# First block's attention: the two score halves of a unit in turn, transposes a unit ahead of values, decay rates held back

## The chip, the core and the metric

The kernel runs on one core of one Trainium2 chip. TensorE multiplies (PE in the profile; PEld is its weight load), VectorE (DVE), ScalarE (ACT) and GpSimd (POOL) work on tiles, SyncE (SP) issues most DMAs. The metric is the device time of one execution in microseconds, as a median of runs.

## What is computed

Two transformer-like blocks over 256 tokens (plus 256 context tokens), in float32. The change touches the first block's attention, which is differential attention with four heads of two 64-wide halves each:

```python
def one_block(q_blk):
    s = jnp.einsum('bhcqd,bhckd->bhcqk', q_blk, k_all).astype(jnp.float32) * scale
    p = jax.nn.softmax(s, axis=-1)
    a = p[:, :, 0] - lam * p[:, :, 1]
    return jnp.einsum('bhqk,bhkd->bhqd', a.astype(v_all.dtype), v_all)
```

The index c is the half (0 or 1). The first block has two layers; layer 0 runs queries of context (256 keys) and of tokens (512 keys), layer 1 those of tokens alone. The change also touches `log_a = -LRU_C * r * jax.nn.softplus(-lam)` of the second block, of which the kernel makes a small constant, the decay rates, ahead of time.

## The kernel before

Every float32 operand of a large product is split into a high and a low part, and `mm3` (L359 to L361) adds three products: high by high, high by low, low by high. Weights come by DMA into `wraw` (four buffers), and `weights` splits them: the high part on ScalarE (L349), the low part on VectorE (L350). The modulation vectors of layer 0 are made from `wmod` weights (two buffers, L337) in steps of products on TensorE (L513); `fill` puts two steps behind each of the first twelve attention units.

A unit of attention is one head and one tile of 128 queries. `scores` takes each half c in turn: its 64 rows of qT and kT are the contraction, so half 0 lies on partitions 0 to 63 and half 1 on 64 to 127. For a half, `mm3` writes one of the two score banks ("sc"), VectorE takes the row maximum (L702), ScalarE the exponential and its sum (L704) into a tile `e` (four buffers). `values` then combines the halves on VectorE (L711 to L713), transposes the result on TensorE (L716), copies it on ScalarE to `aT` (L718), multiplies it by v (L721; each of its float32 products is two instructions), and scales the output (L725, L726). `finish` normalises a head (L732 to L738). The loop calls `scores` of the next unit before `values` of this one. `each` follows every unit: eight taps of the convolution on VectorE (L820), a fill, and now and then a pooling job.

Layer 0 calls `attention` once a head (four units), layer 1 once for two heads (two tiles each, four units); while layer 0's first units run, projections of later heads run too. The order of instructions on each engine isn't the order of the program: a scheduler goes by readiness and priority, and `tc.issue_after(x)` holds instructions behind x in it. `decay` (L920 to L924, with `log_sigmoid` L904 to L915) is called in the hidden stage of layer 1, after tile 10 of 22.

Of the kernel before, what the change touches and what calls it, by code (L numbers as in the profile page):

```python
# [14 lines left out]
AF = mybir.ActivationFunctionType  # L15
ALU = mybir.AluOpType
AX = mybir.AxisListType
# [260 lines left out]
def tile_two_blocks(ctx: ExitStack, tc: tile.TileContext, w: bass.AP, blk: bass.AP, cols: bass.AP,  # L278
# [61 lines left out]
    def weights(key):  # L340
        t, kt, n = raw_chunk(key)
        hi = whi.tile([128, CHUNK], F32R, name="whi")
        lo = wlo.tile([128, CHUNK], F32R, name="wlo")
        m = kt * n
        P["count"] += 1
        if P["both"] and P["count"] % 2:
            dve.tensor_copy(hi[:, :m], t[:, :m])
        else:
            act.copy(out=hi[:, :m], in_=t[:, :m])  # L349
        P["split"] = dve.tensor_tensor(lo[:, :m], t[:, :m], hi[:, :m].bitcast(F32), op=ALU.subtract)  # L350
        v = lambda a: a[:, :m].rearrange("p (k c) -> p k c", k=kt)
        return v(hi), v(lo)
# [5 lines left out]
    def mm3(ps, a, b, start, stop):  # L358
        pe.matmul(ps, a[0], b[0], start=start, stop=False)  # L359
        pe.matmul(ps, a[0], b[1], start=False, stop=False)  # L360
        P["product"] = pe.matmul(ps, a[1], b[0], start=False, stop=stop)  # L361
# [4 lines left out]
    def bank(p):  # L366
        return P[p].tile([128, 512], F32, name="ps_" + p)
# [4 lines left out]
    def st(n=8):  # L372
        return P["wk"].tile([128, n], F32, name=f"st{n}", bufs=8 if n < 64 else 3)
# [313 lines left out]
    def attention(l, h0, qT, kT, v, o, qts, mix, each):  # L687

        lam, sub = coef[l][:2]
        q0 = qts[0]  # L690

        def scores(j, tt):
            nk = 256 if tt < 2 else 512
            mx, s = st(2), st(2)
            e = []
            for c in range(2):
                r = slice(c * 64, c * 64 + 64)
                ps = bank("sc")
                qs = slice((tt - q0) * 128, (tt - q0) * 128 + 128)
                mm3(ps[:, :nk], (qT[j][0][r, qs], qT[j][1][r, qs]), (kT[j][0][r, :nk], kT[j][1][r, :nk]),  # L700
                    True, True)
                dve.tensor_reduce(mx[:, c:c + 1], ps[:, :nk], axis=AX.X, op=ALU.max, negate=True)  # L702
                x = P["wk"].tile([128, 512], F32, name="e", bufs=4)
                act.activation(x[:, :nk], ps[:, :nk], AF.Exp, bias=mx[:, c:c + 1], accum_out=s[:, c:c + 1])  # L704
                e.append(x)
            return nk, s, e

        def values(j, tt, ss, nk, s, e):
            h = h0 + j
            r, cc = st(2), st(1)  # L710
            dve.reciprocal(r, s)  # L711
            dve.scalar_tensor_tensor(cc, s[:, 0:1], r[:, 1:2], lam, op0=ALU.mult, op1=ALU.mult)
            dve.scalar_tensor_tensor(e[0][:, :nk], e[1][:, :nk], cc, e[0][:, :nk], op0=ALU.mult, op1=ALU.add)  # L713
            pt = bank("aux")
            for i in range(nk // 128):
                pe.transpose(pt[:, i * 128:i * 128 + 128], e[0][:, i * 128:i * 128 + 128], ident)  # L716
            aT = P["wk"].tile([128, 512], F32, name="aT", bufs=2)
            act.copy(out=aT[:, :nk], in_=pt[:, :nk])  # L718
            po = bank("aux")
            for i in range(nk // 128):  # L720
                pe.matmul(po[:, :128], aT[:, i * 128:i * 128 + 128], v[i][:, h * 128:h * 128 + 128],  # L721
                          start=(i == 0), stop=(i == nk // 128 - 1))
            q = P["wk"].tile([128, 128], F32, name="sq128")
            i = tt - q0
            act.activation(q, po[:, :128], AF.Square, scale=r[:, 0:1], accum_out=ss[:, i:i + 1])  # L725
            dve.tensor_scalar(o[tt][:, h * 128:h * 128 + 128], po[:, :128], r[:, 0:1], None, op0=ALU.mult)  # L726

        def finish(j, ss):
            h = h0 + j
            n = len(qts)  # L730
            c = slice(h * 128, h * 128 + 128)
            dve.tensor_scalar(ss[:, :n], ss[:, :n], 1.0 / 128, EPS, op0=ALU.mult, op1=ALU.add)  # L732
            rsqrt(ss[:, :n], n)
            for i, tt in enumerate(qts):
                dve.scalar_tensor_tensor(o[tt][:, c], o[tt][:, c], ss[:, i:i + 1], sub, op0=ALU.mult, op1=ALU.mult)
            pt = bank("aux")
            for i, tt in enumerate(qts):
                pe.transpose(pt[:, i * 128:i * 128 + 128], o[tt][:, c], ident)  # L738
            m = slot()
            split(pt[:, :n * 128], m[0][:, :n * 128], m[1][:, :n * 128])  # L740
            mix[h] = m

        units = [(j, tt) for j in range(len(qT)) for tt in qts]
        sums = {j: st(4) for j in range(len(qT))}
        ahead = scores(*units[0])
        for i, (j, tt) in enumerate(units):
            now = ahead
            if i + 1 < len(units):
                ahead = scores(*units[i + 1])
            values(j, tt, sums[j], *now)  # L750
            if tt == qts[-1]:
                finish(j, sums[j])
            each()

    def pooled(l, j, h, seqs, mix):

# [163 lines left out]
    def decay():  # L920

        log_sigmoid(cneg, C("lam2"), 4)
        dve.tensor_scalar(cneg, cneg, 8.0, None, op0=ALU.mult)
        dve.tensor_scalar(cpos, cneg, -1.0, None, op0=ALU.mult)  # L924

    for l in range(DEPTH):
# [27 lines left out]
        def each():  # L954
            run_taps(8)
            if not last and unit[0] < len(FILL):
                fill(FILL[unit[0]])
            unit[0] += 1
            if jobs and unit[0] in POOL_AFTER[l]:
                jobs.pop(0)()  # L960
# [57 lines left out]
        for t, (f0, f1) in enumerate(THIRDS):  # L1018
# [3 lines left out]
            for f in range(f0, f1):  # L1022
                g = scr()
                s = slot()

                def gate(p, g=g):
                    act.activation(g[:, :n], p, AF.Silu)

                def fin(p, g=g, s=s):
                    dve.tensor_tensor(g[:, :n], p, g[:, :n], op=ALU.mult)  # L1030
                    split(g[:, :n], s[0][:, :n], s[1][:, :n])
                items += [(("g", l, f), gate), (("u", l, f), fin)]
                hs.append(s)
                if t == 0 and not last and f == 0:
                    continue
                if t == 0 and not last and f == 1:
                    feats(items[:3], h, [(0, 256), (256, 512)])
                    items = items[3:]
                for it in items:
                    feats([it], h, [(lo, 512)])  # L1040
                items = []
                rows_step(0)
                if last and f == 10:
                    decay()
            final = t == 2
            if final:
                h_next = new_h()
# [629 lines left out]
```

## Time and profile before

| what | us |
|---|---|
| median of 3 runs | 1404.02 |
| lowest and highest of them | 1397.06, 1407.89 |
| the profiled execution's own time | 1406.04 |
| its span, from the first to the last instruction | 1404.2 |
| TensorE busy in it | 1337.7 |

The mean granted TensorE clock of the profiled execution is 0.968 of full speed. Times below are us from the start of its span. Ends of matmuls are modelled, so what a product costs is read from one start to the next.

### The profile page before, as it was taken

What the parts mean: (1) busy time and instruction counts of PE and PEld (TensorE: products, weight loads), DVE (VectorE), ACT (ScalarE), POOL (GpSimd) and SP (SyncE); (2) the same over time, 40 slices, a digit from 0 to 9 for tenths busy, and PEclk for the clock granted to TensorE, in tenths of its full rate; (3) what the DMA queues carried; (4) which work ended last, traced back from release to release, by engine and by line L of the source; (5) the groups of instructions that cost most, each with busy time, mean ns of one, the idle gap of its engine ahead of it and who ended that gap; (6) DMA issues with size and microseconds to landing.
All of it is one profiled execution on the core that took longest, in us unless ns stands there. A gap on an engine that the chain in (4) does not pass through costs nothing.

```text
span 1404.2 us, 22735 instructions
## 1 busy us (share of the span) xinstructions
PE 1337.7 (95%) x8754; PEld 1173.3 (84%) x8754; DVE 965.5 (69%) x1928; ACT 602.9 (43%) x1085; POOL 233.5 (17%) x274
## 2 busy tenths in 40 slices
PE   5899999899999999998988989999999999998999
PEld 2699667798888888888977879999977788998999
DVE  4599766678667767746976655555678677757565
ACT  3333454433222222335344544444565546656443
POOL 0056631310000000013316230000173002000000
PEclk9999999999999999998988889999999999999999
DMA  8424450425444667732321235555564423444553
GB/s 336 178 86 141 161 170 30 151 92 186 157 159 156 196 209 236 237 111 72 109 91 46 81 120 176 195 176 185 168 237 144 152 89 100 149 143 152 186 184 132
DMA packets 61309, 213.53 MB, mean 152 GB/s; under 512 B 6928, under 2 KB 8080, under 8 KB 60944
## 3 DMA queue, kind: packets, MB, share of 16 engines
q1 hardware_dynamic: 60768, 209.91, 44.8%
q10 hardware_dynamic: 432, 2.16, 0.4%
q8 instruction: 69, 1.13, 0.3%
q14 instruction: 40, 0.33, 0.1%
HBM read 211.00 MB, written 1.05 MB: 151 GB/s over the span
## 4 chain that ended last, share of the span: by engine, by line
PE 83%; DVE 6%; ACT 4%; DMA 3%; POOL 2%; issue 2%; SPq 0%; ACTq 0%; POOLq 0%; DVEq 0%
PE ps_mm L359 22%; PE ps_mm L360 22%; PE ps_mm L361 21%; PE ps_sc L359 2%; PE ps_aux L359 2%; DVE wlo L350 2%; PE ps_aux L361 2%; PE ps_aux L360 2%; PE ps_aux L721 1%; PE ps_sc L360 1%; PE ps_sc L361 1%; DVE cacc L820 1%; ACT whi L349 1%; PE ps_md L513 1%; DMA wraw<-in_w_dram 1%
## 5 line engine op out<-in xcount | busy, mean ns | idle before, releaser
L349 ACT CAST whi<-wraw 128x1024 fp32r<-128x1024 f32 (+2 forms) x292 | 300.5, 1033 | 528.6 <-PE ps_mm L360 257.4
L350 DVE TENSOR_TENSOR wlo<-wraw,whi 128x1024 fp32r<-128x1024 f32 (+2 forms) x296 | 356.5, 1206 | 163.4 <-ACT whi L349 160.9
L359 PE MATMUL ps_mm<-hH,whi 128*128 128x256 f32 (+1 forms) x1056 | 344.3, 329 | 11.1 <-ACT hH L497 8.9
L360 PE MATMUL ps_mm<-hL,whi 128*128 128x256 f32 (+1 forms) x1056 | 342.6, 326 | 2.2 <-DVE hL L498 2.2
L361 PE MATMUL ps_mm<-hH,wlo 128*128 128x256 f32 (+1 forms) x1056 | 342.6, 326 | 1.3 <-DVE wlo L350 1.3
L359 PEld LDWEIGHTS ps_mm<-hH,whi 128*128 128x128 f32 x1056 | 204.4, 195 | 32.4 <-ACT hH L497 10.7
L360 PEld LDWEIGHTS ps_mm<-hL,whi 128*128 128x128 f32 x1056 | 204.9, 194 | 19.6 <-DVE hL L498 3.8
L361 PEld LDWEIGHTS ps_mm<-hH,wlo 128*128 128x128 f32 x1056 | 204.6, 194 | 17.7 <-DVE wlo L350 2.5
L359 PE MATMUL ps_mm<-hidH,whi 128*128 128x256 f32 (+1 forms) x683 | 214.1, 316 | 1.7 <-ACT hidH L355 1.7
L360 PE MATMUL ps_mm<-hidL,whi 128*128 128x256 f32 (+1 forms) x683 | 214.4, 315 | 0.0
L361 PE MATMUL ps_mm<-hidH,wlo 128*128 128x256 f32 (+1 forms) x683 | 213.4, 314 | 0.0
L360 PE MATMUL ps_mm<-wlo,hH 128*128 128x256 f32 (+2 forms) x464 | 143.2, 310 | 3.5 <-DVE wlo L350 3.5
L359 PE MATMUL ps_mm<-whi,hH 128*128 128x256 f32 (+2 forms) x464 | 139.9, 310 | 2.1 <-ACT tm L647 1.4
L361 PE MATMUL ps_mm<-whi,hL 128*128 128x256 f32 (+2 forms) x464 | 141.9, 307 | 0.0
L359 PEld LDWEIGHTS ps_mm<-hidH,whi 128*128 128x128 f32 x683 | 129.2, 190 | 10.5 <-ACT hidH L355 1.9
L360 PEld LDWEIGHTS ps_mm<-hidL,whi 128*128 128x128 f32 x683 | 129.8, 190 | 8.9 <-issue 0.5
L361 PEld LDWEIGHTS ps_mm<-hidH,wlo 128*128 128x128 f32 x683 | 129.4, 190 | 8.0
L470 POOL TENSOR_TENSOR squares<-squares,scr 128x256 f32<-128x256 f32 (+1 forms) x28 | 31.6, 1130 | 561.3 <-ACT scr L469 560.8
L580 DVE CUSTOM_DVE_ANT_0 ps_md<-wmod,tm 128x512 f32<-128x512 f32 x160 | 111.5, 697 | 12.4 <-DMA wmod<-in_w_dram 9.7
L848 DVE SCALAR_TENSOR_TENSOR xT<-ps_mm,modv,xT 128x256 f32<-128x256 f32 x116 | 52.5, 479 | 74.1 <-PE ps_mm L361 74.1
L364 POOL TENSOR_TENSOR st<-st,mhalf 128x4 f32<-128x4 f32 (+3 forms) x54 | 65.1, 1209 | 198.8 <-DVE st L632 86.7
L360 PEld LDWEIGHTS ps_mm<-wlo,hH 128*128 128x128 f32 x464 | 88.3, 191 | 9.6 <-DVE wlo L350 5.8
(347 smaller groups left out, 1996.6 us busy)
## 6 DMA issues: line engine op xcount, KB each, us to landing
wraw<-in_w_dram SPq DMA_DIRECT2D x271, 512.0 KB, 3.3
wmod<-in_w_dram SPq DMA_DIRECT2D x85, 512.0 KB, 4.1
wraw<-in_w_dram SPq DMA_DIRECT2D x32, 448.0 KB, 3.2
xT<-in_x_dram ACTq DMA_DIRECT2D x2, 1024.0 KB, 7.0
single<-in_w_dram SPq DMA_DIRECT2D x8, 256.0 KB, 7.5
wraw<-in_w_dram SPq DMA_DIRECT2D x4, 288.0 KB, 3.5
tm<-in_rows_dram SPq DMA_DIRECT2D x4, 256.0 KB, 6.1
out_dram<-scr SPq DMA_DIRECT2D x8, 128.0 KB, 1.7
```

The source lines that it names most:

```text
L349: act.copy(out=hi[:, :m], in_=t[:, :m])
L350: P["split"] = dve.tensor_tensor(lo[:, :m], t[:, :m], hi[:, :m].bitcast(F32), op=ALU.subtract)
L359: pe.matmul(ps, a[0], b[0], start=start, stop=False)
L360: pe.matmul(ps, a[0], b[1], start=False, stop=False)
L361: P["product"] = pe.matmul(ps, a[1], b[0], start=False, stop=stop)
L364: pool.tensor_tensor(t, t, mhalf[:, :n], op=ALU.pow)
L470: eng.tensor_tensor(squares[:, lo:hi], squares[:, lo:hi], q, op=ALU.add)
L513: inst = pe.matmul(ps[g * 32:g * 32 + 32, :256], csil[:, k, :], t[:, g * 256:g * 256 + 256], start=(k == 0), stop=(k == KD - 1), tile_posi ...
L580: dve.tensor_tensor_reduce(bank("md"), t[:, i * 512:i * 512 + 512], crow[2 * j + i], 1.0, 0.0, ALU.mult, ALU.add, sums[j][:, i * KD + d:i ...
L721: pe.matmul(po[:, :128], aT[:, i * 128:i * 128 + 128], v[i][:, h * 128:h * 128 + 128], start=(i == 0), stop=(i == nk // 128 - 1))
L820: dve.scalar_tensor_tensor(av, u[:, j, :n, i:i + 256], colt[:, o + i:o + i + 1], av, op0=ALU.mult, op1=ALU.add)
L848: dve.scalar_tensor_tensor(xT[:, d, r], ps[:, s * 256 - lo:s * 256 - lo + 256], M(l, which, 1 - s)[:, d:d + 1], xT[:, d, r], op0=ALU.mult, ...
```

## The change

`scores` takes both banks at once and issues the six products in turn: the same of the three products for half 0, then for half 1, each held behind the one before by `issue_after`. The reductions follow; the exponentials become `exps`, called later. `values` is cut in two: `turned` combines, transposes and copies, `values` multiplies by v and scales. The loop now keeps scores and exponentials two units ahead, and calls for each i: scores of unit i+2, values of unit i-1 (and finish), turned of unit i, exps of unit i+2, each. `decay` is held behind the last high part and low part of weights at its place in the program.

```diff
@@ -346,7 +346,7 @@
         if P["both"] and P["count"] % 2:
             dve.tensor_copy(hi[:, :m], t[:, :m])
         else:
-            act.copy(out=hi[:, :m], in_=t[:, :m])
+            P["high"] = act.copy(out=hi[:, :m], in_=t[:, :m])
         P["split"] = dve.tensor_tensor(lo[:, :m], t[:, :m], hi[:, :m].bitcast(F32), op=ALU.subtract)
         v = lambda a: a[:, :m].rearrange("p (k c) -> p k c", k=kt)
         return v(hi), v(lo)
@@ -690,23 +690,31 @@
         q0 = qts[0]
 
         def scores(j, tt):
+
             nk = 256 if tt < 2 else 512
             mx, s = st(2), st(2)
+            ps = [bank("sc"), bank("sc")]
+            qs = slice((tt - q0) * 128, (tt - q0) * 128 + 128)
+            for i, (a, b) in enumerate(((0, 0), (0, 1), (1, 0))):
+                for c in range(2):
+                    r = slice(c * 64, c * 64 + 64)
+                    with tc.issue_after(P["product"].ins) if i or c else nullcontext():
+                        P["product"] = pe.matmul(ps[c][:, :nk], qT[j][a][r, qs], kT[j][b][r, :nk], start=i == 0,
+                                                 stop=i == 2)
+            for c in range(2):
+                dve.tensor_reduce(mx[:, c:c + 1], ps[c][:, :nk], axis=AX.X, op=ALU.max, negate=True)
+            return nk, ps, mx, s
+
+        def exps(nk, ps, mx, s):
             e = []
             for c in range(2):
-                r = slice(c * 64, c * 64 + 64)
-                ps = bank("sc")
-                qs = slice((tt - q0) * 128, (tt - q0) * 128 + 128)
-                mm3(ps[:, :nk], (qT[j][0][r, qs], qT[j][1][r, qs]), (kT[j][0][r, :nk], kT[j][1][r, :nk]),
-                    True, True)
-                dve.tensor_reduce(mx[:, c:c + 1], ps[:, :nk], axis=AX.X, op=ALU.max, negate=True)
                 x = P["wk"].tile([128, 512], F32, name="e", bufs=4)
-                act.activation(x[:, :nk], ps[:, :nk], AF.Exp, bias=mx[:, c:c + 1], accum_out=s[:, c:c + 1])
+                act.activation(x[:, :nk], ps[c][:, :nk], AF.Exp, bias=mx[:, c:c + 1], accum_out=s[:, c:c + 1])
                 e.append(x)
             return nk, s, e
 
-        def values(j, tt, ss, nk, s, e):
-            h = h0 + j
+        def turned(j, tt, nk, s, e):
+
             r, cc = st(2), st(1)
             dve.reciprocal(r, s)
             dve.scalar_tensor_tensor(cc, s[:, 0:1], r[:, 1:2], lam, op0=ALU.mult, op1=ALU.mult)
@@ -716,6 +724,10 @@
                 pe.transpose(pt[:, i * 128:i * 128 + 128], e[0][:, i * 128:i * 128 + 128], ident)
             aT = P["wk"].tile([128, 512], F32, name="aT", bufs=2)
             act.copy(out=aT[:, :nk], in_=pt[:, :nk])
+            return nk, r, aT
+
+        def values(j, tt, ss, nk, r, aT):
+            h = h0 + j
             po = bank("aux")
             for i in range(nk // 128):
                 pe.matmul(po[:, :128], aT[:, i * 128:i * 128 + 128], v[i][:, h * 128:h * 128 + 128],
@@ -742,15 +754,21 @@
 
         units = [(j, tt) for j in range(len(qT)) for tt in qts]
         sums = {j: st(4) for j in range(len(qT))}
-        ahead = scores(*units[0])
-        for i, (j, tt) in enumerate(units):
-            now = ahead
-            if i + 1 < len(units):
-                ahead = scores(*units[i + 1])
-            values(j, tt, sums[j], *now)
-            if tt == qts[-1]:
-                finish(j, sums[j])
-            each()
+        n = len(units)
+        held = {i: exps(*scores(*units[i])) for i in range(min(2, n))}
+        turn = {}
+        for i in range(n + 1):
+            ahead = scores(*units[i + 2]) if i + 2 < n else None
+            if i:
+                j, tt = units[i - 1]
+                values(j, tt, sums[j], *turn.pop(i - 1))
+                if tt == qts[-1]:
+                    finish(j, sums[j])
+            if i < n:
+                turn[i] = turned(*units[i], *held.pop(i))
+                if ahead:
+                    held[i + 2] = exps(*ahead)
+                each()
 
     def pooled(l, j, h, seqs, mix):
 
@@ -1041,7 +1059,8 @@
                 items = []
                 rows_step(0)
                 if last and f == 10:
-                    decay()
+                    with tc.issue_after(P["high"].ins), tc.issue_after(P["split"].ins):
+                        decay()
             final = t == 2
             if final:
                 h_next = new_h()
```

## Rows read from the trace of the kernel before

**Rows 1.** Page, part 1: busy us (share of the span) xinstructions of an engine.

```profile
PE 1337.7 (95%) x8754; PEld 1173.3 (84%) x8754; DVE 965.5 (69%) x1928; ACT 602.9 (43%) x1085; POOL 233.5 (17%) x274
```

**Rows 2.** Table of stretches: us, busy us (xinstructions) by engine, PEclk, DMA share, GB/s.

```profile
105.00:155.00 50.00, 49.68 (x388) 42.60 (x387) 46.60 (x89) 21.44 (x49) 31.82 (x33) 1.00 0.41 144
155.00:217.00 62.00, 59.57 (x387) 37.91 (x386) 39.77 (x98) 30.29 (x95) 25.08 (x44) 0.94 0.46 153
717.00:735.00 18.00, 14.22 (x56) 9.49 (x54) 11.67 (x22) 10.57 (x24) 0.00 (x0) 0.72 0.25 82
```

**Rows 3.** Timeline, TensorE, layer 1: start, us, instruction [idle before <-releaser].

```profile
721.84 0.49 PE L359 MATMUL ps_sc<-hidH 64*128 64x512 f32 x1 [2.37 <-ACT e L704]
...
732.22 0.79 PE L359 MATMUL ps_sc<-hidH 64*128 64x512 f32 x1
```

**Rows 4.** Timeline of TensorE, layer 0, where both halves run in turn.

```profile
125.74 0.28 PE L360 MATMUL ps_mm<-wlo,hH 128*128 128x256 f32 x1
125.86 0.28 PE L361 MATMUL ps_mm<-whi,hL 128*128 128x256 f32 x1
126.07 0.39 PE L359 MATMUL ps_sc<-hidH 64*128 64x256 f32 x2
126.29 0.29 PE L360 MATMUL ps_sc<-hidL,hidH 64*128 64x256 f32 x2
...
126.63 0.42 PE L513 MATMUL ps_md<-wmod,csil 128*32 128x256 f32 x4
```

**Rows 5.** Timeline of TensorE: one half with 256, 512, and 512 keys (low clock).

```profile
155.06 0.38 PE L359 MATMUL ps_sc<-hidH 64*128 64x256 f32 x1
...
155.61 0.42 PE L513 MATMUL ps_md<-wmod,csil 128*32 128x256 f32 x4
...
164.11 0.50 PE L359 MATMUL ps_sc<-hidH 64*128 64x512 f32 x1
...
165.00 0.42 PE L513 MATMUL ps_md<-wmod,csil 128*32 128x256 f32 x4
...
727.79 0.79 PE L359 MATMUL ps_sc<-hidH 64*128 64x512 f32 x1
...
729.37 0.58 PE L721 MATMUL ps_aux<-tm,aT 128*128 128x128 f32 x1
```

**Rows 6.** Groups, TensorE, 155:217 us: instruction xcount | busy us, mean ns | idle.

```profile
L513 PE MATMUL ps_md<-wmod,csil 128*32 128x256 f32 x136 | 12.8, 419 | 1.1 <-DMA wmod<-in_w_dram 1.1
L721 PE MATMUL ps_aux<-tm,aT 128*128 128x128 f32 x68 | 10.8, 298 | 0.0
L716 PE MATMUL ps_aux<-first,e 128*128 128x128 f32 x36 | 6.3, 286 | 0.0
```

**Rows 7.** Groups of VectorE and ScalarE in attention, 512 keys, whole span.

```profile
L702 DVE TENSOR_REDUCE st<-ps_sc 128x1 f32<-128x512 f32 x32 | 21.9, 688 | 20.9 <-PE ps_sc L361 20.7
...
L713 DVE SCALAR_TENSOR_TENSOR e<-e,st 128x512 f32<-128x512 f32 x16 | 13.0, 813 | 0.3
...
L704 ACT ACTIVATE e<-ps_sc,st 128x512 f32<-128x512 f32 x32 | 22.1, 690 | 16.1 <-DVE st L702 11.6 <-DVE st L711 4.5
```

**Rows 8.** Timeline of ScalarE near the start.

```profile
41.51 1.28 ACT L905 ACT_TABLE_LOAD   x1
...
42.91 0.35 ACT L518 COPY cp<-ps_sc 128x256 f32<-128x256 f32 x1
```

**Rows 9.** The chain that ended last, near the start: start, us, engine, tile, line.

```profile
45.41 0.15 DVE modv L533 x2
```

**Rows 10.** Table of stretches: layer 1's hidden stage.

```profile
870.00:930.00 60.00, 60.00 (x502) 60.00 (x501) 34.51 (x43) 25.57 (x34) 0.00 (x0) 1.00 0.55 180
```

**Rows 11.** Timeline of TensorE: two of its waits.

```profile
49.98 0.50 PE L360 MATMUL ps_mm<-hL,whi 128*128 128x512 f32 x1 [1.73 <-DVE hL L498]
...
182.12 0.64 PE L513 MATMUL ps_md<-wmod,csil 128*32 128x256 f32 x8 [0.68 <-DMA wmod<-in_w_dram]
```

**Rows 12.** The page, part 6: DMA issues xcount, KB each, median us to landing.

```profile
wmod<-in_w_dram SPq DMA_DIRECT2D x85, 512.0 KB, 4.1
```

## The prediction

> **What bounds the kernel now.** I read the page's engine totals first: TensorE is busy for 1337.7 of 1404.2 us [rows 1]. That is an average, so I went next to a table of stretches around the two places where the first block runs attention. Layer 0 attends between 104 and 228 us. In its two stretches TensorE is busy for 49.7 of 50 and 59.6 of 62 us, at a granted clock of 1.00 and 0.94 of full speed; VectorE has 46.6 of 50 and then 39.8 of 62, ScalarE never half [rows 2]. This stage is bound by TensorE. Layer 1 attends in two groups of four units from 717 us on. In the stretch to 735 the mean clock is 0.72, with VectorE and ScalarE busy for more than half [rows 2]: here TensorE waits, 2.37 us at 721.84 for the exponentials to give back a score bank [rows 3]. That stage is bound by latency. Third I read TensorE's order in time, where the price of the edit stands. The rest of the kernel is not touched; the layer 1 hidden stage has TensorE at 60.00 of 60 us [rows 10], so time won earlier is carried through it.
>
> **Part 1, score products in turn on the two row halves.** Six products make a unit's scores: three for rows 0 to 63, three for rows 64 to 127. Before, they mostly stand as two separate blocks. Three with 256 keys take 155.61 - 155.06 = 0.55 us from the first start to the next other instruction; three with 512 keys take 165.00 - 164.11 = 0.89, and at the low clock 729.37 - 727.79 = 1.58 [rows 5]. Entering such a block costs more: ordinary products follow each other by 0.12 us, the first score product comes 0.21 after its predecessor [rows 4], so 0.09 more. The trace already holds what the new order would give. At 126.07 the scheduler happened to run both halves in turn, and the second group of two lasts 0.29 us together, where one alone lasts 0.28: the two start 0.01 us apart. All six fit into 126.63 - 126.07 = 0.56 us [rows 4], the price of one half. So a unit gives back one whole half block: 0.89 + 0.09 = 0.98 us with 512 keys, 0.55 + 0.09 = 0.64 with 256.
>
> Layer 0 has 16 units; the first two, with 256 keys, already run like this, which leaves 8 of 512 and 6 of 256: 8 x 0.98 + 6 x 0.64 = 11.7 us of TensorE time, the upper bound. How much arrives? A unit also has its transposes, its values and, in twelve of sixteen, two steps of the modulation products. By rows [rows 6] those are 4 x 6.3/36 = 0.70, 8 x 10.8/68 = 1.27 and 16 x 12.8/136 = 1.51 us with 512 keys, so TensorE needs about 5.4 us per unit before and 4.4 after. Both banks of a new unit are now taken together and are free only after the second exponential: 0.89 for the products, two reductions of 0.69 one behind the other on VectorE, one exponential of 0.69 [rows 7] give 2.96 us. That hides behind 4.4, but not where the modulation steps are missing (4.4 - 1.5 = 2.9). The FILL table has none for the last head, so I count nothing for its four units: 11.7 - (2 x 0.98 + 2 x 0.64) = 8.5 us. The lower bound is 3.1, worked out in the first rival.
>
> The Trainium skill (TensorEngine Tiling (Array Packing), Performance Considerations, "PSUM Bottleneck") warns that tiling speeds up TensorE but not the emptying of PSUM, which may then be the bottleneck. If that held in all of layer 0, the 8.5 would be nearer to 0 and the total nearer to 1400; with TensorE's 4.4 us against the banks' 2.96 the trace bears it out for the last head alone.
>
> In layer 1 eight units with 512 keys run; the first of each group is paired already. There the second unit's first half starts at 721.84 and the fourth unit's second half at 732.22 [rows 3]: 10.4 us for three units, 3.46 each, much of it products at the low clock. The new cycle of 2.96 saves half a microsecond on each of six units: 3.0 us. Bounds: 0, if the banks are the cycle already, and 6 x 1.58 = 9.5, if each second half was on the path at the low clock.
>
> **Part 2, transposes a unit ahead of values.** No instruction is added or removed. `turned` of unit i no longer has its `values` right behind it, so the copy between them is covered by the next scores. Where TensorE is busy that copy was already covered by other work, so I count 0 in layer 0, and in layer 1 leave it inside the 3.0. What is late next: the exponentials of unit i+2 go into the buffers of unit i (four are there), so they now wait until that unit's transposes are done, and stand on ScalarE behind its copy. `each`, with two DMAs for modulation weights a unit, comes before the unit's own values: the same loads in the same order on SP's queue, a little sooner.
>
> **Part 3, decay kept late.** Before, the scheduler had pulled `decay` to 41 us. There ScalarE loads a table for 1.28 us while the copy of the modulation sums waits behind it until 42.91 [rows 8], and VectorE runs over a dozen tiny instructions before it adds the bias at 45.41 [rows 9]; TensorE then idles 1.73 us for hL [rows 11]. The table is still wanted, by `layer_scalars` right behind the copy. At most the load's 1.28 us and about half of VectorE's 45.41 - 42.91 - 0.35 = 2.15 us behind the copy fall off the path, together 2.4 us; at least none, if the instructions for lambda take their place and wait for the same table. I take 1.5. In its new place (the third hidden tile of the second third of layer 1, near 909 us) it brings two table loads and two tiny activations, 3.0 us of ScalarE, and two dozen VectorE instructions of 0.17, 4 us. In 60 us there ScalarE is idle for 34 and VectorE for 25 [rows 10], and three buffers of split weights lie ahead. I count 0; without that cover, 3.0.
>
> **Sum.** -8.5 - 3.0 - 1.5 + 0 = -13.0 us. The profiled execution took 1406.04 us (span 1404.2), so it would take 1393; it lies 2.0 above the median of the runs shown (1404.02), so I forecast a median of 1391.
>
> **Rivals.**
> 1. *The loads of modulation weights set the pace.* Two buffers, 4.1 us from issue to landing [rows 12] and some 0.75 us of products a step: two steps cannot come much faster than every 4 to 5 us, and at 182.12 TensorE already waited 0.68 us for one [rows 11]. Against it: 17 steps in 62 us leave 3.6 us a step on average. If it holds, the 256-key units win nothing, the six 512-key units before the last head win 5.9, four more waits of 0.7 take 2.8 of that, and layer 1 wins nothing: 1404 - 3.1 - 1.5 = 1399. Chance 0.22.
> 2. *The queues keep the written order (slower).* On VectorE the reductions of unit i+2 are written ahead of the combining (L713) of unit i. If they are issued so, a unit is one chain: products 0.89, reductions 1.38, combining 0.81, transposes 0.70, exponentials 1.38, and only then the next products: 5.2 us with 512 keys against 5.4; the copy behind the transposes, the small instructions and the way from engine to engine, five times, add some 1.5 (an estimate). At +1.3 us for the 14 units of layer 0 and 1.5 for the eight of layer 1 (no other work to fill): 1404 + 18 + 12 - 1.5 = 1432 at full price, about 1420 with half of it filled. It decides when L713 of a unit stands behind both L702 of the unit two later. Against it: L713's inputs are ready a whole unit earlier, and the scheduler goes by what is ready. Chance 0.10.
> 3. *TensorE gets thinner and its clock falls in layer 0,* as it does in layer 1 with the same attention [rows 2]. 52 us at 0.72 instead of 0.94 cost 16 us: 1404 + 16 - 13 = 1407. Against it: projections and modulation steps fill layer 0. Chance 0.08.
> 4. *The pairs don't overlap,* because other products get between them. Then only one entry a unit and one exit of the same 0.09 fall away, 14 x 0.18 = 2.5: 1404 - 2.5 - 1.5 = 1400. The 0.01 us of [rows 4] speaks against it. Chance 0.03.
> 5. *Everything arrives:* 11.7 + 6 (two thirds of the upper bound in layer 1) + 2.4 gives 1384 or a little less. Chance 0.13.
>
> **How the numbers follow.** My forecast, 1391 with its own range of 1386 to 1396, has 0.44. A difference of 1%, 14 us, is about what a measurement of this kernel can tell from no change. 1391 lies just inside it, so I split the forecast 0.24 faster and 0.20 same. Faster: 0.24 + 0.13 = 0.37. Same: 0.20, rivals 1 and 4 with 0.25, rival 3 mostly (0.06) and a little of rival 2 (0.02), 0.53. Slower: 0.08 + 0.02 = 0.10. For 8 in 10 the range leaves out rival 2 and the end of rival 5 and takes in rival 3: 1383 to 1407.
>
> **What would show it.** Step 1: score products in groups of six with 0.56 or 0.9 us to the next instruction, pairs 0.01 us apart. If their time falls and the stretch 105 to 217 shrinks by less than 6 us, look at the waits for the wmod loads (rival 1) and for the exponentials (rival 2). Layer 1: the wait of 2.37 us stays, the distance from unit to unit falls to 3.0. Part 3: no decay near 41 us, hL's first wait shorter, TensorE still full near 909. The forecast is wrong if VectorE or ScalarE instructions of attention end most TensorE waits in layer 0, or if layer 0's clock drops below 0.9.

## The result, and the profile after

The changed kernel takes 1422.15 us (median; 1420.23 to 1426.51), before 1405.95 beside it. The ratio is 1.0122, 95% interval 1.0089 to 1.0155: 1.2% slower, where I had forecast 1391 with a range to 1407. The profiled execution takes 1420.61 us (span 1418.8), its span 14.6 longer than the 1404.2 of before. Lines of after: L702 are the score products, L705 the reductions, L712 the exponentials, L719 to L721 the combining (reciprocal, factor, weighted difference, L711 to L713 before), L724 the transposes, L726 the copy behind them, L733 the values.

The page's engine totals of after (answers [rows 1]): TensorE is busy for 8.5 us less, and the kernel is longer.

```profile
PE 1329.2 (94%) x8754; PEld 1165.9 (82%) x8754; DVE 961.3 (68%) x1928; ACT 609.0 (43%) x1089; POOL 235.0 (17%) x274
```

Timeline of TensorE in layer 0, after (answers [rows 5]): start, us, instruction.

```profile
167.96 0.50 PE L702 MATMUL ps_sc<-hidH 64*128 64x512 f32 x2
168.29 0.40 PE L702 MATMUL ps_sc<-hidL,hidH 64*128 64x512 f32 x2
168.53 0.39 PE L702 MATMUL ps_sc<-hidH,hidL 64*128 64x512 f32 x2
168.85 0.70 PE L800 MATMUL ps_mm<-scr,colt 128*128 128x256 f32 x2
```

All six products take 168.85 - 167.96 = 0.89 us, what three took: here the pairs do what the forecast said. But of the 14 units of layer 0 that were to gain, only 4 run so in after, and 5 in e1, e5 and e9 (runs below). In the others the first product of half 0 starts alone, other products come between, and the remaining five follow later. Timeline of TensorE in e9:

```profile
132.98 0.50 PE L701 MATMUL ps_sc<-hidH 64*128 64x512 f32 x1
133.41 0.38 PE L360 MATMUL ps_mm<-wlo,hH 128*128 128x256 f32 x1
...
133.96 0.50 PE L701 MATMUL ps_sc<-hidH 64*128 64x512 f32 x1
...
134.85 1.07 PE L513 MATMUL ps_md<-wmod,csil 128*32 128x256 f32 x16
```

The lone product takes 133.41 - 132.98 = 0.43 us, the five 134.85 - 133.96 = 0.89, as much as six, and the block is entered twice. Such a unit gives back about half of what the forecast counted.

To see where the time goes, I compare executions at equal points of the work: the start of the copy that splits the nth weight tile (296 tiles, same order in every kernel). Lead (-) or lag against before, us:

| kernel | 13th (before: 102.4) | 91st (615.1) | 127th (835.4) | 295th (1390.3) |
|---|---|---|---|---|
| after | -3.4 | +6.2 | +14.7 | +14.6 |
| e1 pairs alone | -1.2 | -5.4 | -1.8 | -2.2 |
| e2 loop alone | -0.8 | +5.4 | +16.1 | +15.5 |
| e3 after, six e buffers | -2.1 | -6.8 | +0.6 | +1.4 |
| e4 decay alone | -2.6 | -2.8 | -9.3 | -9.4 |
| e5 pairs in layer 0, decay | -3.0 | -6.3 | -6.6 | -6.3 |
| e6 after, combining first | -2.4 | -5.3 | -4.4 | -4.9 |
| e9 pairs, decay | -0.2 | -4.7 | -1.2 | -0.4 |
| e13 pairs in layer 1, decay | -1.7 | +2.0 | +5.4 | +5.8 |

Layer 0's attention lies between the first two columns, layer 1's between the next two. After loses 9.6 us in layer 0, where I expected -8.5, and 8.5 in layer 1, where I expected -3.0; the start gives 3.4. Outside these three places it loses nothing. The step from the second column to the third flatters every kernel beside before: ahead of layer 1's attention, between the 91st and the 109th tile, before's own trace is 3.5 to 5.4 us longer than the others' (e14 aside). TensorE waits there 2.2 us for L800, a wait that is at most 0.7 us elsewhere. So layer 1's attention is better compared from the 109th to the 124th tile.

Table of stretches, both attentions between the same two weight tiles (13th to 27th, 109th to 124th), so the same work in each: us, busy us (xinstructions) of PE, PEld, DVE, ACT, POOL, then PEclk, DMA share, GB/s. Before:

```profile
102.42:260.41 157.99, 153.56 (x981) 116.07 (x980) 115.36 (x244) 71.08 (x179) 64.04 (x83) 0.96 0.36 123
711.39:830.15 118.76, 101.08 (x638) 87.33 (x637) 77.18 (x157) 56.73 (x127) 41.06 (x53) 0.84 0.22 71
```

After:

```profile
99.00:267.31 168.31, 150.69 (x981) 114.39 (x980) 112.20 (x244) 72.75 (x180) 63.94 (x83) 0.94 0.34 115
714.11:844.84 130.73, 98.95 (x639) 85.19 (x638) 78.46 (x162) 56.79 (x127) 41.20 (x53) 0.83 0.19 65
```

TensorE's idle time (first number less the second) rises from 4.4 to 17.6 us in layer 0 and from 17.7 to 31.8 in layer 1.

What it waits for is told by the exponentials with 512 keys. Group of after, ScalarE: busy, mean ns | idle before them and what ended it.

```profile
L712 ACT ACTIVATE e<-ps_sc,st 128x512 f32<-128x512 f32 x32 | 22.1, 692 | 29.5 <-DVE e L721 19.3 <-DVE st L719 5.7 <-DVE st L705 4.4
```

Before, the wait of 16.1 us was for the unit's own reductions and for L711 [rows 7]; now 19.3 of 29.5 are for the combining L721, a step of the unit two earlier. Timeline of VectorE in layer 1, after, units 1 and 2 of a group (counted from 0):

```profile
727.77 1.29 DVE L705 TENSOR_REDUCE st<-ps_sc 128x1 f32<-128x512 f32 x2 [2.20 <-PE ps_sc L702]
731.29 0.69 DVE L705 TENSOR_REDUCE st<-ps_sc 128x1 f32<-128x512 f32 x1 [2.23 <-PE ps_sc L702]
731.89 0.15 DVE L719 RECIPROCAL st<-st 128x2 f32<-128x2 f32 x1
731.97 0.67 DVE L705 TENSOR_REDUCE st<-ps_sc 128x1 f32<-128x512 f32 x1
732.55 0.21 DVE L720 SCALAR_TENSOR_TENSOR st<-st,st,lam 128x1 f32<-128x1 f32 x1
732.80 0.75 DVE L721 SCALAR_TENSOR_TENSOR e<-e,st 128x512 f32<-128x512 f32 x1
```

And of ScalarE: the last accumulator read of unit 0, and the two exponentials of unit 2.

```profile
726.25 0.20 ACT L712 ACTIVATION_READ_ACCUMULATOR e<-ps_sc,st 128x1 f32 x1
...
733.65 0.69 ACT L712 ACTIVATE e<-ps_sc,st 128x512 f32<-128x512 f32 x1 [3.70 <-DVE e L721]
...
734.82 0.59 ACT L726 COPY aT<-ps_aux 128x512 f32<-128x512 f32 x1 [0.40 <-PE ps_aux L724]
735.30 0.69 ACT L712 ACTIVATE e<-ps_sc,st 128x512 f32<-128x512 f32 x1
```

Of TensorE, the next score products (unit 3) and the values between them:

```profile
734.71 0.79 PE L702 MATMUL ps_sc<-hidH 64*128 64x512 f32 x1
735.46 2.08 PE L733 MATMUL ps_aux<-tm,aT 128*128 128x128 f32 x8
737.47 0.79 PE L702 MATMUL ps_sc<-hidH 64*128 64x512 f32 x1
```

Unit 0's sums are there at 726.45. VectorE runs unit 1's reductions, stands idle for 2.23 us, and still combines unit 0 only from 731.89 on: in its queue that stands behind the reductions of unit 2, which wait for unit 2's scores. The exponentials of unit 2 have their maxima at 731.98 and 732.64, and run at 733.65 and 735.30, since the e tiles they write are still those of unit 0. The first of the next score products starts at 734.71, when the first of these exponentials has run; the other five follow at 737.47, behind the values. That is the chain of rival 2.

### The profile page after: what moved, and what is told of

It is laid out like the page before. It is cut to its first block, busy times and chain, and to the rows that moved or that the text cites. A ratio compares the mean times of both kernels' runs of the same rounds, so it can differ in the third digit from the quotient of the medians.

```text
span 1418.8 us, 22744 instructions
## 1 busy us (share of the span) xinstructions
PE 1329.2 (94%) x8754; PEld 1165.9 (82%) x8754; DVE 961.3 (68%) x1928; ACT 609.0 (43%) x1089; POOL 235.0 (17%) x274
## 4 chain that ended last, share of the span: by engine, by line
PE 82%; DVE 7%; ACT 4%; issue 3%; POOL 3%; DMA 2%; ACTq 0%; POOLq 0%; DVEq 0%
PE ps_mm L359 22%; PE ps_mm L360 22%; PE ps_mm L361 22%; PE ps_aux L733 2%; PE ps_aux L359 2%; PE ps_aux L361 2%; PE ps_aux L360 2%; DVE wlo L350 1%; PE ps_sc L702 1%; DVE cacc L838 1%; DMA wraw<-in_w_dram 1%; ACT whi L349 1%; PE ps_sc L359 1%; PE ps_aux L1458 1%; PE ps_md L513 1%
## 5 line engine op out<-in xcount | busy, mean ns | idle before, releaser
L361 PEld LDWEIGHTS ps_mm<-hH,wlo 128*128 128x128 f32 x1056 | 203.2, 193 | 17.5 <-DVE wlo L350 2.3
```

## Experiments on the loop

All ratios are to before, with 95% intervals.

**e1, pairs alone** in before's loop:

```
-  per half: three products, reduction, exponential
+  six products in turn into two banks; then reduction, exponential per half
```

> Only the product order is changed: the six score products go in turn into both banks; the reductions, the exponentials and the loop (one unit ahead, values right behind the transposes) stay as before, and decay stays early. Theory 1 (the new loop order costs the time: exponentials two units ahead find no free e buffer until the transposes of the unit two earlier are done, and these stand behind that unit's combining on VectorE): the pairs alone keep what they save, so 1394 to 1402 us against 1406 before, with the stretch 105 to 217 us shorter by 3 to 10 us. Theory 2 (taking both score banks together costs the time, since the next six products wait for the second exponential): slower than before by the 19.6 us that the loop and pairs together cost in the changed kernel (16.2 by the medians plus 3.4 from decay), about 1425, with waits of score products for e (the exponential) as in the changed kernel.

Measured: 1405.05 us, ratio 0.9984 (0.9959 to 1.0009). No 20 us lost, so theory 2 falls as the main cause. But the gain is smaller than theory 1 wanted: 4.2 us won in layer 0, 3.6 lost in layer 1 (table).

**e2, the loop alone**, halves as before:

```
-  P["product"] = pe.matmul(ps[c]..., in turn over c
+  mm3(ps[c][:, :nk], ...) per half, then its reduction
```

> Only the loop is changed: scores two units ahead, exponentials after the transposes of the unit two earlier, values a unit behind; the products of a half stay together in one bank, as before, and decay stays early. Theory 1 (loop order): 1424 to 1434 us, that is before plus the whole 19.6 us or more, since the saving of the pairs is missing too. Theory 2 (both banks held together by the pairs): 1400 to 1410.

Measured: 1421.81 us, 1.0124 (1.0067 to 1.0181). The loop alone makes the loss.

**e3, six e buffers:**

```
-  x = P["wk"].tile([128, 512], F32, name="e", bufs=4)
+  x = P["wk"].tile([128, 512], F32, name="e", bufs=6)
-  aT = P["wk"].tile([128, 512], F32, name="aT", bufs=2)
+  aT = e[1]
```

> The changed kernel with six e buffers in place of four (the copy of the transposes goes into the second e tile of its unit, so that two buffers come free and the space stays the same). The exponentials of unit i+2 then need the buffers of unit i-1 and no longer wait for the transposes of unit i. Theory 1a (the e buffers close the chain): most of the 19.6 us comes back, 1400 to 1408, and the waits of exponentials for DVE e (3.70 us at 729.95 to 733.65 in the changed kernel) are gone. Theory 1b (the order on VectorE alone, reductions ahead of combining, sets it): less than a third comes back, 1416 to 1422. Theory 2 (banks held by the pairs): 1420 to 1424, no change.

Measured: 1407.64 us, 1.0011 (0.9984 to 1.0038), 14.5 below after. Group of e3, ScalarE: the wait for L721 is gone, that for the unit's own reductions is 17.5 us (11.6 before).

```profile
L712 ACT ACTIVATE e<-ps_sc,st 128x512 f32<-128x512 f32 x32 | 22.0, 688 | 17.6 <-DVE st L705 17.5
```

**e6, combining first,** four buffers as in after:

```
   for i in range(n + 1):
+      if i < n:
+          both = turned(...)      # L719 to L721 of unit i
       ahead = scores(*units[i + 2]) ...
       values of unit i - 1
-      turn[i] = turned(...)
+      turn[i] = flipped(*both)    # transposes and copy of unit i
       held[i + 2] = exps(*ahead)
```

> The changed kernel with VectorE's combining of unit i (reciprocal, factor, weighted difference) written ahead of the scores and reductions of unit i+2; the e buffers stay four, transposes, values and exponentials keep their order. Theory 1b (the order on VectorE makes the chain, as in rival 2 of the prediction): the transposes of unit i start earlier, the exponentials of unit i+2 too, and 5 to 14 us come back, 1408 to 1417. Theory 1a (the four e buffers alone, whatever VectorE's order): 1419 to 1423, no change, since the exponentials still wait for the transposes of unit i.

Measured: 1402.80 us, 0.9980 (0.9963 to 0.9998), 19.4 below after, more than either theory expected. Timeline of VectorE in the same place of e6:

```profile
714.80 1.29 DVE L705 TENSOR_REDUCE st<-ps_sc 128x1 f32<-128x512 f32 x2 [2.06 <-PE ps_sc L702]
716.01 0.16 DVE L719 RECIPROCAL st<-st 128x2 f32<-128x2 f32 x1
716.20 0.22 DVE L720 SCALAR_TENSOR_TENSOR st<-st,st,lam 128x1 f32<-128x1 f32 x1
716.45 0.75 DVE L721 SCALAR_TENSOR_TENSOR e<-e,st 128x512 f32<-128x512 f32 x1
718.31 1.29 DVE L705 TENSOR_REDUCE st<-ps_sc 128x1 f32<-128x512 f32 x2 [1.11 <-PE ps_sc L702]
```

Unit 0 is combined at 716.01, ahead of unit 2's reductions at 718.31. Group of ScalarE, and stretches of e6:

```profile
L712 ACT ACTIVATE e<-ps_sc,st 128x512 f32<-128x512 f32 x32 | 22.0, 691 | 16.9 <-DVE st L705 13.4 <-DVE e L721 3.5
```

```profile
100.02:255.75 155.73, 145.13 (x981) 110.97 (x980) 111.83 (x244) 70.72 (x179) 63.08 (x83) 0.97 0.37 125
701.30:825.74 124.44, 99.31 (x644) 86.27 (x643) 79.08 (x162) 56.59 (x126) 42.04 (x53) 0.85 0.21 68
```

Against after, layer 0 is 12.6 us shorter: 7.0 of idling (17.6 to 10.6) and 5.6 of TensorE's busy time (150.7 to 145.1; same instructions, clock 0.97 for 0.94). Layer 1 is 6.3 shorter.

**e7, both mends,** e3's edit in e6:

> The two together: combining written first, and six e buffers (copy of the transposes in the second e tile). With six buffers alone it was 1407.6 us. If what was left of the loss there is the order on VectorE: 1400 to 1404. If it is the pairs in layer 1 (8 us by the run of pairs alone): no change, 1405 to 1409.

Measured: 1407.69 us, 1.0004 (0.9981 to 1.0027). The mends don't add: each opens the same chain. The 4.9 us that six buffers cost beside e6 lie within the two intervals; a possible cause, not tested here, is that the copy into e's second tile holds that tile until the values are done (e8 below has the same copy).

**e12, the whole of combining, transposes and copy first:**

```
+      turn[i] = turned(...)
       held[i + 2] = exps(*scores(*units[i + 2]))
       values of unit i - 1
```

> The changed kernel with the whole of a unit's combining, transposes and copy written ahead of the scores of the unit two later, and the values after these. Theory 1b: the combining is again ahead of the reductions, so it comes out like combining first, 1400 to 1405. If the place of the transposes and exponentials matters more than that of the combining: it differs from 1402.8 by more than 4 us, either way. Theory 1a alone (four e buffers, no matter who is first) would leave it at 1418 to 1423.

Measured: 1407.50 us, 1.0012 (0.9986 to 1.0037): 15 below after, 4.7 above e6. The combining's place decides most; what the rest of the order is worth can't be told, since the intervals of e12 and e6 overlap.

**e10, combining first without pairs** (e2's products in e6):

> The mended loop (combining first, four buffers, decay late) with the products of a half together, as before. The difference to the 1402.8 us of the run with combining first is what the pairs are worth in this loop. If they are worth what TensorE's work says (9.7 us less work in layer 0, some of it lost to waits): 1407 to 1412. If they are worth nothing: 1401 to 1405. If the order on VectorE is the whole loss of the new loop (theory 1b), it is in any case at least 8 us below the run of the loop alone (1421.8), after 3 to 5 for decay are taken off.

Measured: 1401.89 us (1397.12 to 1416.16), 1.0009 (0.9972 to 1.0045). Against e2 it is 19.9 us less by medians, 16 by the ratios (1.0124 - 1.0009); with 3 to 5 taken off for decay, at least 11 are left for the order, with halves apart too. Against e6 the pairs are worth nothing by medians and 4 us by the ratios, within the intervals. The executions of e10 spread widely.

## Experiments on pairs and decay

**e9, pairs and decay late** in before's loop, the change without its new loop:

> Pairs in both layers and decay late, in before's loop (one unit ahead): the change without its new loop. The mended loop with combining first stood at 1402.8 us. If two units ahead and the transposes ahead of values are worth nothing by themselves (part 2 of the prediction): the same, 1400 to 1404. If they are worth something once the chain is open: 1405 or more here. By adding the single runs (pairs minus 2.9, decay minus 6.5 by medians) it would be 1397.

Measured: 1404.56 us, 0.9996 (0.9974 to 1.0019). With e6 at 0.9980, two units ahead and transposes ahead are worth nothing that can be told: part 2's 0 holds once the chain is open, as far as these intervals tell.

**e5, pairs in layer 0 alone** (`if l:` keeps the halves apart), decay late:

> Before's loop; the six products go in turn in layer 0 alone (layer 1 keeps its halves apart, as before); decay kept late. From the runs of pairs alone and of decay alone: the pairs are worth 4.2 us in layer 0 (lead 1.25 us at the 12th weight tile, 5.4 from the 24th on), and cost about 8 us in layer 1; decay is worth 2.8 to 5. Theory 2 for layer 1 (taking both banks together costs where the banks set the pace): 1397 to 1400, with layer 1 attention as long as before (116 to 119 us between the same two weight tiles, against 126.4 with pairs). If the loss in layer 1 has another cause, such as an earlier arrival there: 1402 to 1406.

Measured: 1400.95 us, 0.9972 (0.9956 to 0.9989), but layer 1 took 123.56 us at clock 0.82, not the 116 to 119 expected, with unchanged code. TensorE's instructions of layer 1 stand in another order there than in before or e4: the build orders them anew when other code changes.

**e13, pairs in layer 1 alone,** decay late:

> Before's loop, decay late, pairs in layer 1 alone (the mirror of the run with pairs in layer 0 alone). If pairs in layer 1 cost what the runs with pairs in both layers showed: layer 1's stretch between the same two weight tiles is 124 to 127 us at a clock near 0.81 (116.6 to 118.8 with halves apart), and the whole 1406 to 1410. If layer 1 is longer in those runs for another reason, such as the order that the build gives it after a changed layer 0: 116 to 120 us, and 1400 to 1403.

Measured: 1410.00 us, 1.0021 (0.9984 to 1.0059). Table of stretches, layer 1 of e13:

```profile
709.20:835.20 126.00, 102.34 (x631) 87.95 (x630) 79.73 (x163) 56.59 (x126) 45.12 (x56) 0.80 0.21 67
```

As expected of pairs, 126 us; e1, e8, e9 and e15 have 125.9 to 127.8. With halves apart it was 118.8 (before), 116.6 (e4), 118.4 (e11) and 123.6 (e5).

**e11, a third score bank in layer 1** (halves apart, decay late):

```
-  ps = bank("sc")
+  ps = bank("md" if l and (4 * j + 2 * (tt - q0) + c) % 3 == 2 else "sc")
```

> Decay late and a third score bank in layer 1 alone (the modulation's bank is free there): every third half goes into it, everything else as before. Theory 2 for layer 1 (two score banks set the pace there, 2.96 us a unit with pairs and 3.46 without, by the prediction): the waits of score products for the exponential (1.59 and 0.93 us near 716 in the run of decay alone) go, and layer 1's stretch between the same two weight tiles falls from 116.6 us by 3 to 6: about 1397. If something else sets it (low clock, the copies and transposes at the end of a group): 1400 to 1403, as decay alone.

Measured: 1400.40 us, 0.9984 (0.9958 to 1.0011), layer 1 118.41 us: no gain over e4. The score products of a group of four units now start within 9.0 and 9.4 us (15.6 and 13.4 in e4), and the stretch is no shorter. With halves apart, two banks don't set the pace.

**e14, four banks for pairs in layer 1:**

```
-  ps = [bank("sc"), bank("sc")]
+  spare = l and (tt - q0) % 2
+  ps = [bank("md" if spare else "sc"), bank("mm" if spare else "sc")]
```

> Pairs in both layers, decay late, before's loop; in layer 1 every second unit takes its two score banks from the modulation's bank and one of the three projection banks, so that a unit need not wait for the exponentials of the unit before. If both banks held together are what pairs cost in layer 1: the waits of score products for the exponential (1.59, 1.18, 1.37 and 1.23 us in the run of pairs with decay) go, and the stretch falls from 126.4 to 119 to 122 us, total near 1399. If it is not the banks: 125 to 128 and 1403 to 1407.

Measured: 1407.35 us, 0.9999 (0.9965 to 1.0033). Groups of TensorE, layer 1 (700 to 790 us), e9 and then e14:

```profile
L701 PE MATMUL ps_sc<-hidH 64*128 64x512 f32 x16 | 9.4, 681 | 6.9 <-ACT e L707 5.6 <-ACT hidH L355 1.3
...
L671 PE MATMUL ps_aux<-first,tm 128*128 128x128 f32 x16 | 3.6, 357 | 4.4 <-DVE hidL L356 4.2 <-DVE tm L659 0.2
```

```profile
L671 PE MATMUL ps_aux<-first,tm 128*128 128x128 f32 x16 | 3.8, 318 | 12.6 <-DVE tm L659 12.4 <-DVE hidL L356 0.2
L702 PE MATMUL ps_sc<-hidH 64*128 64x512 f32 x8 | 3.3, 568 | 1.9 <-ACT e L708 1.5 <-ACT hidH L355 0.2
```

In the score banks the wait for exponentials falls from 5.6 to 1.5 us, and the units in the other two banks have none, but the transposes of queries and keys now wait 12.4 for L659. The banks taken away from the projections confound it, so it doesn't show whether held banks are the whole price: between the 91st and the 127th tile e14 loses 5.0 us, more than e9.

**e8 and e15, a third buffer for modulation weights** with pairs: `wmod=3` for 2, paid in e8 (decay early) by `aT = e[1]`, in e15 (decay late) by `hid=8` for 9:

> Pairs alone in before's loop, decay early, with three buffers for modulation weights in place of two (the copy of the transposes goes into the second e tile, whose place pays for it). In the run of pairs alone TensorE gained 9.7 us of work in layer 0 and lost 5.8 to idling, of which five waits for wmod loads make 5.0. If the two load buffers set that pace (rival 1 of the prediction): the waits for wmod in 140 to 220 us vanish, 4 to 5 us more gained in layer 0, about 1400. If the DMA queues' rate sets it: the waits stay, 1404 to 1406. A shorter start is possible too, since the first modulation uses the same buffers; it would show before 60 us.

> Pairs in both layers, decay late, before's loop, three buffers for modulation weights, paid by one of nine hidden slots; nothing in attention's own buffers is changed. If the load buffers take back half of what the pairs save in layer 0 (five waits for wmod, 5.3 us, in the run of pairs with decay): these waits go and the stretch of layer 0 falls from 152.7 to 148 to 150 us. If the next wait takes their place: 152 us and more, as with the copy in the second e tile (159.8).

Measured: e8 1413.13 us, 1.0050 (1.0025 to 1.0075); e15 1405.00, 0.9987 (0.9953 to 1.0020). Groups of TensorE in layer 0 (140 to 216 us), e9 and then e15:

```profile
L513 PE MATMUL ps_md<-wmod,csil 128*32 128x256 f32 x160 | 12.6, 389 | 5.6 <-DMA wmod<-in_w_dram 5.5
L701 PE MATMUL ps_sc<-hidH 64*128 64x512 f32 (+1 forms) x26 | 10.2, 457 | 2.5 <-ACT e L707 2.4
```

```profile
L513 PE MATMUL ps_md<-wmod,csil 128*32 128x256 f32 x160 | 12.6, 405 | 0.5 <-DMA wmod<-in_w_dram 0.5
L701 PE MATMUL ps_sc<-hidH 64*128 64x512 f32 (+1 forms) x25 | 9.9, 457 | 3.9 <-ACT e L707 3.9
```

Stretches of layer 0, e9 and then e15:

```profile
102.19:254.84 152.65, 142.38 (x981) 110.05 (x980) 112.52 (x244) 71.10 (x180) 64.66 (x83) 0.99 0.37 127
```

```profile
99.51:253.63 154.12, 146.38 (x981) 112.45 (x980) 112.73 (x244) 70.86 (x179) 65.31 (x83) 0.96 0.36 123
```

The loads' wait goes, 5.5 to 0.5 us, and idling falls from 10.3 to 7.7 us; yet the stretch isn't shorter: the banks' wait grows by 1.5, and the same products take 4.0 us more at a clock of 0.96 for 0.99. That e8 is 9 us slower than e1 by the ratios, clear of both intervals, isn't due to the third buffer alone, since e15 has it too; beside decay and the hidden slot, e8 differs from e15 in the copy into the second e tile.

**e4, decay alone late, and e16, after with decay early:**

> Only decay is kept late, with the waits of the change; everything else as before. By the two traces the changed kernel is 3.4 us ahead from 60 to 120 us and loses nothing near 909 us. If that is decay alone: 1402.5 us, ratio 0.9976. If the lead has another cause (the first units' attention runs in the same stretch): 1405 to 1406. My prediction said minus 1.5.

> The changed kernel with decay back in its early place and without its two waits. By my prediction decay is worth 1.5 us: 1423 to 1424. By the single run of decay alone 5.2: 1427. By the two traces 3.4: 1425.5. If decay is worth nothing, 1422.

Measured: e4 1401.40 us, 0.9963 (0.9936 to 0.9990); e16 1426.70, 1.0131 (1.0057 to 1.0205) against after's 1.0122. Decay late is worth 5.2 us by e4, 1.3 by e16, and -1.7 by e9 against e1, each uncertain by several: about 1.5 fits, its size isn't settled. The traces mislead here: the 13th tile leads by 2.6 in e4 and 0.2 in e9, both with decay late, but TensorE's clock in 41 to 66 us was 1.00 in the one and 0.93 in the other (0.93 in before).

Four runs in before's loop with decay late differ only in where the pairs are: nowhere (e4, 0.9963), in layer 0 (e5, 0.9972), in layer 1 (e13, 1.0021), in both (e9, 0.9996). Averaged over the other layer, pairs in layer 0 are worth 1.1 us and pairs in layer 1 cost 5.8, each give or take 3.8 (an estimate from the four intervals).

No version is clearly better than all: decay alone (0.9963), e5 (0.9972) and e6 (0.9980) beat before by 0.2 to 0.4%.

## Why the prediction was wrong, step by step

**Part 2, the step that failed.** I wrote "I count 0" for the loop, and saw that the exponentials of unit i+2 "now wait until that unit's transposes are done"; I did not follow what these wait for. That was in rival 2, with its condition: L713 of a unit behind both L702 of the unit two later. The trace of after has it (731.29, 731.89, 731.97, 732.80). I gave it 0.10 since "the scheduler goes by what is ready". It doesn't on this queue: VectorE idles 2.23 us with unit 0's combining ready behind. Its price was 18 + 12 at full and about half of it with other work to fill; e6 against after says 19.4. The half was a guess, so that the result lies near rival 2's 1420 is partly luck; the mechanism is not.

**Part 1, layer 0: too large in work, and idle time grows.** Expected: 11.7 us less TensorE time, of which 8.5 arrive. The busy time is 153.56 before, 143.9 in e1 and 142.4 in e9, but the clock of these two was 0.98 and 0.99, for 0.96 before. At before's clock, in e15, it is 146.38: 7.2 us less. I had priced all 14 units as blocks of six; in e9 five run so. Nine run as one product and five, which saves 0.98 - 0.43 - 0.09 = 0.46 us with 512 keys and 0.64 - 0.31 - 0.09 = 0.24 with 256 (there the lone product takes 154.65 - 154.34 = 0.31 us in e9). That makes 4 x 0.98 + 0.64 + 4 x 0.46 + 5 x 0.24 = 7.6 us, an estimate from e9's starts. Rival 4's condition, other products between, held there for the first product alone. And I took idle time as constant. In e9 it grows from 4.4 to 10.3 us, 5.5 of these for wmod loads (1.3 before in the same stretch of time): rival 1, partly. So 3.3 to 4.5 us arrive between the 13th and the 91st tile (e1, e5, e9, e15). Even that depends on the clock: with halves apart in before's loop the same stretch lies between 0.3 less (e4) and 5.9 us more (e11).

**Part 1, layer 1: wrong sign.** Forecast -3.0; from the 109th to the 124th tile the kernels with pairs in before's loop (e1, e8, e9, e13, e15) take 7 to 9 us more than before. My step compared a cycle of 2.96 us a unit with one of 3.46, and had both wrong. The 3.46 ran from the second unit's first half to the fourth unit's second half; from start to start it is 724.40 - 721.84 = 2.56 and 727.79 - 724.40 = 3.39. The 2.96 priced the products at 0.89, their time at full clock, in a stretch that I had read at 0.72 and with 1.58 at the low clock in [rows 5]. Timeline of TensorE, before:

```profile
724.40 0.79 PE L359 MATMUL ps_sc<-hidH 64*128 64x512 f32 x1 [0.82 <-ACT e L704]
```

And e9, the same three starts in the first group, then the last two in the second:

```profile
714.99 1.46 PE L701 MATMUL ps_sc<-hidH 64*128 64x512 f32 x2 [1.59 <-ACT e L707]
...
718.48 1.46 PE L701 MATMUL ps_sc<-hidH 64*128 64x512 f32 x2 [1.18 <-ACT e L707]
...
722.05 0.79 PE L701 MATMUL ps_sc<-hidH 64*128 64x512 f32 x1 [0.22 <-ACT e L707]
...
764.96 0.50 PE L701 MATMUL ps_sc<-hidH 64*128 64x512 f32 x1 [1.37 <-ACT e L707]
...
770.73 1.22 PE L785 MATMUL ps_mm<-scr,colt 128*128 128x256 f32 x2 [1.34 <-POOL scr L784]
...
773.59 0.79 PE L701 MATMUL ps_sc<-hidH 64*128 64x512 f32 x1
```

With pairs the first group's steps are 3.49 and 3.57 us, at a clock of 0.50; with halves apart at 0.50 (e4) they are 3.24 and 3.30. So a unit gains nothing. In the second group the last unit starts 6.9 to 8.6 us after the one ahead of it (e1, e9, e13, e15), against 2.8 in before and e4 and 3.8 in e5: in e9 it stands on TensorE behind L785, which waits for GpSimd. With halves apart the banks weren't the pace, as e11 shows. With pairs score products wait 5.6 us for exponentials in e9, for 3.2 in before. That agrees with the Trainium skill (TensorEngine Tiling (Array Packing), Performance Considerations, "PSUM Bottleneck"), which the prediction held to be borne out for one head alone. Lower clock (0.80 to 0.81 for 0.84 in before) eats the work saved. How much of the loss is banks and how much the build's other order stays open.

**Part 3.** -1.5 fits, within what the runs can tell; the new place costs nothing, as said. Table of stretches of after, where decay now runs:

```profile
904.00:930.00 26.00, 26.00 (x219) 26.00 (x218) 17.30 (x41) 14.35 (x20) 0.00 (x0) 1.00 0.57 185
```

**Rival 3.** The clock in layer 0 was 0.94, not far below 0.96. At that clock busy time makes 5.6 of the 12.6 us between after and e6; since the clock also differs between executions of the same code (0.96 in e4, 0.93 in e11), no run shows that the change lowered it.

## What to carry to other kernels

When a loop is made to run further ahead, write down for each engine the order of its queue, and put the steps that finish an old unit ahead of those that begin a new one: a ready instruction behind a waiting one waits too. Count the buffers with it: two units ahead with two units of buffers means that the new unit waits for the old unit's whole tail. Work taken off a full engine is worth only what the next limit (here loads, score banks, the clock) lets through, so price that limit first, at the clock of the stretch. And count in the trace how often the pattern that was priced appears, not only that it appears.

## What the runs showed of the hardware

TensorE's granted clock varied between executions with the same work. Layer 0 is the same code in e4 and e11. Table of stretches of layer 0, between the same two weight tiles, e4 and then e11:

```profile
99.87:257.58 157.71, 153.58 (x981) 116.33 (x980) 115.05 (x244) 71.15 (x179) 63.92 (x83) 0.96 0.36 123
```

```profile
102.52:265.59 163.07, 158.05 (x981) 118.51 (x980) 115.21 (x244) 71.21 (x179) 63.95 (x83) 0.93 0.35 119
```

The clock also lay low where the engine was full. Table of stretches of e10, layer 0: TensorE is busy for 18.97 of 20 us at 0.88, then for all of 20 us at 0.61.

```profile
185.00:205.00 20.00, 18.97 (x114) 12.80 (x113) 12.84 (x34) 9.06 (x28) 10.15 (x13) 0.88 0.49 169
205.00:225.00 20.00, 20.00 (x110) 12.10 (x109) 8.65 (x23) 8.41 (x27) 0.58 (x1) 0.61 0.33 107
```

So a single trace tells a few microseconds of a stretch only when the clock stands beside it. With pairs in layer 0 the times were in one run much closer together (e5: 1399.07 to 1402.94) than before's beside them (1397.90 to 1416.45); in e1 they were less so (1400.43 to 1412.82, for 1398.66 to 1415.63), so it isn't shown that the pairs do it.
